# Expert weights in two-row pieces, features in a strided order, in a two-block transformer kernel

## The chip, the cores and the metric

The kernel runs on one core of a Trainium2 chip. The metric is the device time of one execution in microseconds (us), the median of several runs.

## The reference, cut to what matters

A first block (two layers with three mixing branches) is followed by a second block, whose last part is a layer of 16 experts. Each expert takes the 64 tokens (`cap = 2 * 512 / 16`) that the router likes best. All arithmetic is float32; the 16 experts' three 1024 x 1024 matrices are 201 MB.

```python
def expert_choice_ffn(h, w_router, w_gate, w_up, w_down):
    ...
    aff = jax.nn.softmax((h @ w_router).astype(jnp.float32), axis=-1)
    gates, idx = lax.top_k(aff.transpose(0, 2, 1), cap)
    xe = h[bidx, idx]
    hg = jnp.einsum('becd,edf->becf', xe, w_gate)
    hu = jnp.einsum('becd,edf->becf', xe, w_up)
    y = jnp.einsum('becf,efd->becd', jax.nn.silu(hg) * hu, w_down)
    y = y * gates[..., None].astype(y.dtype)
    return jnp.zeros_like(h).at[bidx, idx].add(y)
```

## The kernel before, in words

A planner of the language orders each engine's instructions and places the buffers; the kernel's text gives priorities and dependences. The change touches the last stage, `emit_moe`, which runs eight rounds (`q`), each with two experts (`e`). A round has these steps:

- The one-hot matrix (L1364, DVE) marks which token sits in which of the 128 slots of the pair.
- The gather (L1375, TensorE) multiplies it with the residual stream: for each block `k` of 128 features, four products, one for each tile of tokens. The stationary operand is `K.x[t][:, 128 columns]`, the moving one is the one-hot matrix. ACT (L1378) writes the result to `xe`, scaled by `n2` and shifted by `modc`, both per feature.
- `ffn` (L1387) is called for gate, up and down. For each `k` and each `e` it takes one tile of weights, 128 rows of the matrix, one row on a partition (4 KB each, 512 KB a tile), as moving operand. The stationary operand is 64 columns wide, so that expert 0 fills one half of the array's columns and expert 1 the other. In the code's order the two column halves `hf` of expert 0 come first, then those of expert 1.
- Four transposes for each half of the hidden layer (L1403) give `aT`, the stationary operand of the down products.
- The scatter (L1418) multiplies with the transposed one-hot matrix and adds to the output.

One float32 product is recorded as two weight loads (PEld) and two matmuls (PE), so a call of `ffn` has 32 products and 64 records, a gather 32 products and 64 records. The transposes have one record each.

The weights come on SP's queue from `wm` (L214, and through `wraw`, L173). The first 8 tiles (`NE`) have places of their own, the rest go round a ring of 28 tiles (`NW` 4 in `wring`, `NM` 24 in six tiles `wm0` to `wm5`), all 512 KB each. A place is loaded again when the products that read it are done.

Two older lines matter for reading the trace. `tm` (L743 to L753) makes token-major products from the transposed rows `hT`: `tm(0, ...)` takes 128 neighbouring columns as stationary operand, `tm(1, ...)` (L783) every fourth column, `slice(t, None, 4)`; nothing else differs between the two. `Mod.group` (L918) has four strips `j` of the array's columns with one product each, strip by strip in the code.

## Time and profile before

| | us |
|---|---|
| median of 3 runs | 2271.3 (2269.49 to 2281.24) |
| span of the profiled execution | 2273.9 |
| of it, the eight rounds of the experts, from the first gather | 494.2 |
| one round in the middle | 61.75 |

In the rows below, PE is TensorE's matmuls, PEld its weight loads, DVE, ACT and POOL the other engines, SPq the queue on which SP issues transfers. `out<-in` are the program's names for tiles, `x60` is a count, "idle before" is how long the engine had nothing to do and who ended that. A matmul record is longer than the step from one to the next, since matmuls are pipelined: rates are read from the start times.

### The profile page before, as it was taken

Reading aid. Unit: us, or ns where it says so; the run is one execution under the profiler, and the core shown is the slowest. Engines: PE = TensorE matmul, PEld = TensorE weight load, DVE = VectorE, ACT = ScalarE, POOL = GpSimd, SP = SyncE. Lnnn points to the kernel's source line nnn. Section 1 sums busy time; section 2 is a strip of 40 time slices with the busy share of each in tenths; the row PEclk is TensorE's granted clock in tenths of the full one; section 3 lists DMA queues with packets and bytes.
Section 4 is the critical chain, followed back from the end, with each engine's and each line's share of the span. In section 5 each row is a group of like instructions: output and inputs, shape, how many; then the busy total and the mean of one; then the engine's idle time right before and its main releaser. Section 6 shows DMA issues by size and latency. Waiting matters only on the chain. (4 is left out here: it accounts for less than half of the span.)

```text
span 2273.9 us, 31807 instructions
## 1 busy us (share of the span) xinstructions
PE 2128.9 (94%) x12273; PEld 1439.3 (63%) x12273; DVE 1258.6 (55%) x2406; ACT 980.0 (43%) x1849; POOL 429.6 (19%) x344
## 2 busy tenths in 40 slices
PE   6998999999999899999899999999999799999999
PEld 6754667668886676668767777676677444444443
DVE  5688855655569877645867474757464322222221
ACT  4454545444544464444577584857532011101110
POOL 2132233112222323202141140323110000000000
PEclk9999999899999999999999999999999799999999
DMA  6254251043321111034210202011146699999996
GB/s 203 84 171 146 77 168 57 18 158 107 94 87 38 38 38 47 22 124 153 73 51 31 73 20 75 24 61 43 52 157 257 263 401 409 409 409 409 409 409 267
DMA packets 114335, 348.48 MB, mean 153 GB/s; under 512 B 19820, under 2 KB 20604, under 8 KB 114184
## 3 DMA queue, kind: packets, MB, share of 16 engines
q1 hardware_dynamic: 110152, 340.51, 40.7%
q10 hardware_dynamic: 4032, 5.95, 0.8%
q8 instruction: 97, 1.59, 0.3%
q14 instruction: 54, 0.44, 0.1%
HBM read 332.70 MB, written 10.56 MB: 151 GB/s over the span
## 5 line engine op out<-in xcount | busy, mean ns | idle before, releaser
L193 POOL TENSOR_TENSOR wL<-wring,wH 128x1024 fp32r<-128x1024 f32 x68 | 167.2, 2459 | 702.0 <-ACT wH L190 498.8
L190 ACT ACTIVATE wH<-wring 128x1024 fp32r<-128x1024 f32 x137 | 144.1, 1059 | 133.5 <-PE bm L199 96.5
L1387 PE MATMUL bm<-wm,xe 128*64 128x512 f32 x848 | 185.4, 593 | 0.0
L199 PE MATMUL bm<-hT0H,wH 128*128 128x512 f32 x380 | 158.7, 418 | 2.9 <-ACT wH L190 2.9
L199 PE MATMUL bm<-hT1L,wH 128*128 128x512 f32 x380 | 159.8, 421 | 0.0
L199 PE MATMUL bm<-hT0L,wH 128*128 128x512 f32 x380 | 159.6, 420 | 0.0
L199 PE MATMUL bm<-hT0H,wL 128*128 128x512 f32 x380 | 158.6, 417 | 0.0
L199 PE MATMUL bm<-hT1H,wL 128*128 128x512 f32 x380 | 156.5, 412 | 0.0
L199 PE MATMUL bm<-hT1H,wH 128*128 128x512 f32 x380 | 156.0, 411 | 0.0
L1387 PEld LDWEIGHTS bm<-wm,xe 128*64 128x64 f32 x848 | 75.2, 136 | 106.4 <-issue 99.6
L193 DVE TENSOR_TENSOR wL<-wring,wH 128x1024 fp32r<-128x1024 f32 x69 | 92.2, 1337 | 74.4 <-ACT wH L190 66.4
L344 DVE TENSOR_TENSOR Z<-bz,perm 128x512 f16<-128x512 f32 x168 | 108.6, 684 | 36.7 <-PE bz L323 35.6
L1364 DVE TENSOR_SCALAR OH<-phA,perm 128x64 f32<-128x64 f32 x128 | 30.2, 309 | 136.4 <-PE bz L1375 105.7
L1387 PE MATMUL bm<-wm,aT 128*64 128x512 f32 x432 | 102.3, 602 | 0.7
L354 ACT ACTIVATE XX<-bz 128x512 f16<-128x512 f32 x168 | 101.3, 610 | 3.6 <-PE bz L323 3.6
L323 PEld LDWEIGHTS <-XX 128*128 128x128 f16 x1008 | 63.6, 99 | 59.5 <-issue 27.9
L351 ACT ACTIVATE XX<-bz 128x512 f16<-128x512 f32 x140 | 85.2, 608 | 16.7 <-PE bz L323 14.9
L199 PEld LDWEIGHTS bm<-hT0H,wH 128*128 128x128 f32 x380 | 72.8, 192 | 19.4 <-issue 4.2
L199 PEld LDWEIGHTS bm<-hT0L,wH 128*128 128x128 f32 x380 | 72.6, 191 | 17.5 <-issue 5.7
L199 PEld LDWEIGHTS bm<-hT1L,wH 128*128 128x128 f32 x380 | 71.9, 189 | 18.2 <-issue 5.9
L199 PEld LDWEIGHTS bm<-hT1H,wL 128*128 128x128 f32 x380 | 71.9, 189 | 18.1 <-issue 5.3
L199 PEld LDWEIGHTS bm<-hT0H,wL 128*128 128x128 f32 x380 | 72.6, 191 | 15.5 <-issue 3.3
(815 smaller groups left out, 4922.6 us busy)
## 6 DMA issues: line engine op xcount, KB each, us to landing
wm<-in_w_up SPq DMA_DIRECT2D x112, 512.0 KB
wm<-in_w_down SPq DMA_DIRECT2D x108, 512.0 KB
wm<-in_w_gate SPq DMA_DIRECT2D x100, 512.0 KB
wring<-in_win SPq DMA_DIRECT2D x95, 512.0 KB
wring<-in_w_ada SPq DMA_DIRECT2D x48, 512.0 KB
wring<-in_w_gate SPq DMA_DIRECT2D x20, 512.0 KB
wring<-in_w_down SPq DMA_DIRECT2D x20, 512.0 KB
wring<-in_w_out SPq DMA_DIRECT2D x16, 512.0 KB
```

The source lines that it names most:

```text
L190: d = self.A.activation(out=hi, in_=t, func=AF.Copy)
L193: (eng or self.V).tensor_tensor(out=lo, in0=t, in1=hi.bitcast(F32), op=ALU.subtract)
L199: self.T.matmul(out, a[i], b[j], start=(start and n == 0), stop=(stop and n == 2))
L323: T.matmul(b[:, u], lhs[:, u], rhs if len(rhs.shape) == 2 else rhs[:, u], start=True, stop=True)
L344: V.tensor_tensor(out=z, in0=mm(HL[j][0], X[j]), in1=lv(systems[j], l, 0), op=ALU.mult)
L351: A.activation(out=X[j], in_=mm(XT[j], Z[j]), func=AF.Copy)
L354: A.activation(out=XT[j], in_=b, func=AF.Copy)
L1364: V.tensor_scalar(out=y[:, t, 64 * e:64 * e + 64], in0=K.c("iota")[:, 1:65], scalar1=slot[:, t, x:x + 1], scalar2=scale(t, x), op0=ALU.is_ ...
L1387: T.matmul(bb[hf][s], lhs[:, k, s], w[:, hf * 512:(hf + 1) * 512], start=(k == 0), stop=(k == 7))
```

## The change

A transfer of expert weights now brings 256 rows: partition `p` gets two adjacent rows of the matrix (8 KB in one piece, 1 MB a transfer). Of each half of 512 rows, partition `p` holds the rows `4p` to `4p + 3`, the first two in one transfer and the other two in the next. So a block of features `k` is no longer 128 neighbouring features but every fourth one of a half: the gather's stationary operand and the transposes' input are read with a step of four elements. The scale and shift of `xe` are fetched in that order by four small transfers into `nx`, with one DVE operation. In `ffn` a tile now holds two blocks `k`, and the loops are `k0`, `e`, `k`, `hf`, so all eight records of expert 0 come ahead of the eight of expert 1. The ring keeps its bytes: half as many places, twice as large. Comments and docstrings go.

```diff
-NW = 4
+NR = 4
+NW = 2
...
-NM = 24
-NM1 = 8
-NC = 4
-NE = 8
+NM = 12
+NM1 = 4
+NC = 2
+NE = 4
...
     def wm(self, src, pool):
...
-            t = pool.tile([128, 1024], F32, name="we", bufs=NE)
+            t = pool.tile([128, 2, 1024], F32, name="we", bufs=NE)
         elif j < 0:
-            return self.wraw(src)
+            t = self.wring[:, 2 * (j + NW):2 * (j + NW) + 2]
         else:
             if first and j % NC == 0:
-                self.wms = getattr(self, "wms", []) + [pool.tile([128, NC, 1024], F32, name="wm%d" % (j // NC))]
+                self.wms = getattr(self, "wms", []) + [pool.tile([128, NC, 2, 1024], F32, name="wm%d" % (j // NC))]
...
+    nx = K.small("n2x", 24).rearrange("p (j k) -> p j k", j=3)
+    for j, o in enumerate((4096, 3072)):
+        for h in range(2):
+            nc.sync.dma_start(nx[:, j, 4 * h:4 * h + 4], K.mod.flat[:, o + 512 * h:o + 512 * h + 512].rearrange("o (p k) -> (o p) k", k=4))
+    V.scalar_tensor_tensor(out=nx[:, 2], in0=nx[:, 0], scalar=1.0, in1=K.v2[:, _V2["n2x"][0]:_V2["n2x"][0] + 8], op0=ALU.add, op1=ALU.mult)
...
+    strided = lambda k: slice(512 * (k // 4) + k % 4, 512 * (k // 4) + 512, 4)
...
-                    T.matmul(b[:, j], K.x[t][:, (k0 + j) * 128:(k0 + j + 1) * 128], OH[:, t], start=(t == 0), stop=(t == 3))
+                    T.matmul(b[:, j], K.x[t][:, strided(k0 + j)], OH[:, t], start=(t == 0), stop=(t == 3))
...
-                A.activation(out=xe[:, k], in_=b[:, j], func=AF.Identity, scale=n2[:, k:k + 1], bias=modc[:, 24 + k:25 + k])
+                A.activation(out=xe[:, k], in_=b[:, j], func=AF.Identity, scale=nx[:, 2, k:k + 1], bias=nx[:, 1, k:k + 1])
...
-            for k in range(8):
+            for k0 in range(0, 8, 2):
                 for e in range(2):
-                    w = K.wm(a[name][2 * q + e, k * 128:(k + 1) * 128], P2["wm"])
+                    rows = a[name][2 * q + e, 512 * (k0 // 4):512 * (k0 // 4) + 512].rearrange("(p k) n -> p k n", k=4)
+                    w = K.wm(rows[:, k0 % 4:k0 % 4 + 2], P2["wm"])
                     s = slice(64 * e, 64 * e + 64)
-                    for hf in range(2):
-                        T.matmul(bb[hf][s], lhs[:, k, s], w[:, hf * 512:(hf + 1) * 512], start=(k == 0), stop=(k == 7))
+                    for k in (k0, k0 + 1):
+                        for hf in range(2):
+                            T.matmul(bb[hf][s], lhs[:, k, s], w[:, k - k0, hf * 512:(hf + 1) * 512], start=(k == 0), stop=(k == 7))
...
-                T.transpose(b[:, j], hid[hf][:, j * 128:(j + 1) * 128], K.ident)
+                T.transpose(b[:, j], hid[hf][:, j::4], K.ident)
```

## Rows read from the trace of the kernel before

**Rows 1.** Busy time by engine over three rounds; last columns: clock, DMA share, GB/s.

```profile
1779.67:1842.38 62.71, 61.17 (x290) 31.80 (x291) 13.37 (x35) 6.11 (x13) 0.00 (x0) 0.95 0.71 277
...
2025.27:2087.02 61.75, 59.99 (x285) 27.19 (x285) 13.09 (x31) 6.10 (x13) 0.00 (x0) 1.00 1.03 409
...
2210.52:2273.90 63.38, 57.88 (x236) 23.74 (x236) 15.31 (x23) 2.83 (x5) 0.00 (x0) 1.00 0.71 282
```

**Rows 2.** DMA view, 1900 to 2200 us: total, and the queue with the weights.

```profile
DMA packets 33642, 122.69 MB, mean 409 GB/s; under 512 B 3732, under 2 KB 3732, under 8 KB 33624
...
q1 hardware_dynamic: 33624, 122.45, 102.4%
```

**Rows 3.** Waits, 1850 to 2200 us: total us, times, longest.

```profile
PEld bm L1387 <- DMA wm<-in_w_down: 1.6, 7, 0.2
...
PEld bm L1387 <- DMA wm<-in_w_up: 0.7, 3, 0.2
...
PEld bm L1387 <- DMA wring<-in_w_down: 0.2, 1, 0.2
```

**Rows 4.** Timeline of PE, one round: start us, us, operation, count, idle before.

```profile
2025.27 7.11 PE L1418 MATMUL bg<-yg,oT 128*128 128x512 f32 x16 [0.90 <-DVE yg L1409]
...
2046.09 13.96 PE L1387 MATMUL bm<-wm,xe 128*64 128x512 f32 x64
2060.80 1.25 PE L1403 MATMUL bt<-perm,hid 128*128 128x128 f32 x8 [0.76 <-DVE hid L1398]
...
2068.24 1.94 PE L1387 MATMUL bm<-wm,aT 128*64 128x512 f32 x8
2070.11 1.60 PE L1375 MATMUL bz<-OH,x 128*128 128x128 f32 x12
2071.65 1.94 PE L1387 MATMUL bm<-wm,aT 128*64 128x512 f32 x8
```

**Rows 5.** Timeline of SP's queue: the last weights, and one row fetched earlier.

```profile
1771.72 0.33 SPq L245 DMA_DIRECT2D gt<-modb  x1
...
2232.21 9.28 SPq L214 DMA_DIRECT2D wm<-in_w_down  x8
```

**Rows 6.** Chain that ended last: its last three pieces of `ffn`.

```profile
2217.62 27.71 PE bm L1387 x128
2247.45 1.94 PE bm L1387 x8
2249.98 12.26 PE bm L1387 x56
```

**Rows 7.** Timeline of PEld: `tm(1)`, every fourth column; one load a row.

```profile
54.06 0.33 PEld L199 LDWEIGHTS bm<-wH,hT0H 128*128 128x128 f32 x1
...
57.56 0.33 PEld L199 LDWEIGHTS bm<-wH,hT0H 128*128 128x128 f32 x1
```

**Rows 8.** Timeline of PEld: `tm(0)`, neighbouring columns; one load a row.

```profile
30.02 0.19 PEld L199 LDWEIGHTS bm<-wH,hT0H 128*128 128x128 f32 x1
...
31.79 0.19 PEld L199 LDWEIGHTS bm<-wH,hT1H 128*128 128x128 f32 x1
```

**Rows 9.** Timeline of PEld: the second round's gather, 59 loads in a row.

```profile
1842.22 6.67 PEld L1375 LDWEIGHTS bz<-OH,x 128*128 128x128 f32 x59 [0.24 <-issue]
```

**Rows 10.** Timeline around the first round's gather, all engines.

```profile
1760.20 1.74 DVE L1324 SCALAR_TENSOR_TENSOR perm<-lg,perm 128x16 f32<-128x16 f32 x8 [0.78 <-PE lg L1300]
...
1779.67 10.08 PE L1375 MATMUL bz<-OH,x 128*128 128x128 f32 x64 [0.98 <-DVE OH L1364]
1783.46 0.81 ACT L1378 ACTIVATE xe<-bz,perm 128x128 f32<-128x128 f32 x2 [18.15 <-PE bz L1375]
...
1789.67 2.85 PE L1387 MATMUL bm<-we,xe 128*64 128x512 f32 x12
```

**Rows 11.** Timeline of PE: one step of the modulation's products.

```profile
137.87 1.04 PE L918 MATMUL bm<-wring,perm 128*1 128x512 f32 x8
```

## The prediction

> **What bounds the kernel now.** I began with the clock and the busy shares by stage, since the change touches only the eight rounds of the experts, 494.2 us of 2273.9. In a middle round TensorE is busy for 59.99 of 61.75 us at full clock, and the transfers run at 409 GB/s with all engines taken [rows 1]. Both look full, so the busy shares don't say which one sets the pace. Three other views do. The DMA view says the rate is steady at 409 GB/s over 300 us [rows 2]: a round's 48 tiles, 25.17 MB, need 25.17 / 0.409 = 61.5 us, almost exactly the round. The waits say that in 350 us TensorE waited for weights 11 times, 2.5 us in all, never over 0.2 us [rows 3]. And at the end the last weights are issued by 2241.5 us [rows 5], while the last call of `ffn` runs from 2247.45 to 2262.2 [rows 6]: TensorE is behind the transfers, not ahead. So TensorE sets the pace; transfers follow by a hair. The timeline of one round shows what fills it: scatter 7.11, `ffn` for gate and up 13.96 each, 0.90 and 0.76 idle, transposes 1.25, then down and the next gather in turns [rows 4]. Whatever makes TensorE's work longer lengthens the round; what shortens the transfers finds nobody waiting.

> **Faster transfers.** Half as many transfers, pieces of 8 KB for 4 KB. No row has such pieces for weights, so their rate is bounded by what it can do: a faster rate gains at most the 2.5 us of [rows 3], which I book as a gain, since a longer round also gives it. A slower rate costs nothing until 25.17 MB take longer than the new round, below 25.17 / 69.4 = 363 GB/s. The ring keeps its bytes. A place comes free after 1 MB of work, later than now, but the first weights lie ready long before the first gather.

> **The gather's stationary operand, every fourth column.** The trace has this very form elsewhere: `tm(1)` loads 128 columns with a step of four floats, `tm(0)` 128 neighbouring ones, all else alike. In `tm(1)` 15 loads take 57.56 - 54.06 = 3.50 us, 0.233 us each, recorded as 0.33 [rows 7]. In `tm(0)` 15 loads take 1.77 us, 0.118 each, recorded as 0.19 [rows 8]. The gather has 0.19 us loads too, 59 of them in 6.67 us, so (6.67 - 0.19) / 58 = 0.112 us each [rows 9]. Its matmuls are as short as the step, so nothing covers a longer load: I take 0.233 for 0.112, 0.121 us more on each of 64 loads, 7.8 us a round. For the seven rounds after the first: 7 x 64 x 0.121 = 54.2 us. The first gather runs partly at half clock and takes 10.08 us [rows 1, 10]; 64 x 0.233 = 14.9 gives +4.8, and +9.8 if its first 21 loads take double. All of this is on TensorE, which sets the pace.

> [...]

> **Transposes.** Eight a round have the hidden layer with a step of four as stationary operand; now they take 1.25 us [rows 4]. No row shows a strided transpose. The bounds are nothing and the same 0.233 for each: 8 x 0.233 = 1.87, with a tail of 0.2 some 2.05, +0.8 a round and +6.4 in all. I take the upper end, since it is the same kind of load. They stand alone between up and down, so it counts fully.

> **Order and turns in `ffn`.** Eight records of `ffn` between two pieces of gather take 1.87 us from start to start, a piece of gather of 12 takes 1.54 [rows 4]. Undisturbed, 8 records take 13.8 / 64 x 8 = 1.73 and 12 loads 1.34: one turn costs 0.14 + 0.20 = 0.34 us. Five rounds have such turns, 8 pieces of down each. With two blocks a tile I expect 4 pieces, 4 x 0.34 x 5 = 6.8 us less; if the planner keeps the pieces it is 0. I take half, -3.4.

> The 64 records in 13.96 us also show that expert 0's and expert 1's records run side by side on the two halves of the columns: a record alone takes 0.44 (16 in 7.11) [rows 4], so 64 in a row would take 28. Yet the code has four of expert 0, then four of expert 1, so the array starts expert 1's over three waiting ones. Now eight stand ahead. Rows 11 show 8 records on four strips in 1.04 us, four at once, though the fourth strip's first stands six places behind the first strip's: it reaches that far at least. I take 0 for the new order; the other end is the second rival.

> If matmuls could start only in the order of the code, expert 1's first could run beside expert 0's eighth at the earliest: 14 steps of 0.43 us for each 16 records where 8 do now, 2.6 us on each of 96 pairs of tiles, +248 us. The records that overtake others in [rows 4, 11] speak against it.

> [...]

> **The four small transfers and their users.** They go on SP's queue, behind weights: a row of the modulation now leaves at 1771.72 [rows 5]. ACT's `xe` waits for them, and behind it `ffn`. The first `xe` runs at 1783.46 and `ffn` starts at 1789.67 after the gather [rows 10]; the gather, which gets longer, hides them. I take 0. If the DVE operation were queued ahead of the router's chain, which starts at 1760.20 [rows 10], DVE would wait up to the transfers' landing near 1780, and the one-hot matrix and gather behind it: +20.

> **Sum.** 54.2 + 4.8 + 6.4 - 3.4 - 2.5 = 59.5 us, 2333.4 for the profiled 2273.9. The median of the runs is 2.6 lower, 2271.3, so 2331. The bounds: 54.2 + 4.8 - 6.8 - 2.5 = 49.7 below (transposes free) and 54.2 + 9.8 + 6.4 = 70.4 above. The planner may order the earlier stages a little differently; I allow 5 us either way, for which no row stands: 2316 to 2347.

> **Rivals.** First, on the other side: the load's second half is hidden, because the gather's loads are the two parts of plain float32 and those of `tm` are not, or because the array fetches them ahead. Then TensorE keeps its rounds, and only the turns and waits change: 2271.3 - 9.3 = 2262, at worst 2271. It decides if the new gather's loads stay under 0.112 us. For it: both forms record 0.19 us unstrided. Against: that likeness says that they read alike, and `tm`'s matmuls, whose step is 0.118, did not hide 0.233. Chance 0.09; half hidden, near 2300, 0.06.

> Second: the two experts no longer run fully side by side. If the array reaches no further than the six places of rows 11, expert 1 starts two records late, 0.86 us, at each of five starts a round: 40 x 0.86 = +34, 2365. If the planner puts gather between expert 0's eight and expert 1's, down takes 28 for 14 us in five rounds: +69, 2400. Chance 0.17 together. The strict order above, 2580, has 0.03.

> Third: the DVE operation stalls the router's chain, 2351. Chance 0.03. That transfers in pieces fall below 363 GB/s and bound the round, 0.02.

> **How the numbers follow.** The forecast, 2331, has 0.60. From 2305 to 2395 lie the forecast with its bounds, the third rival and most of the second: some 0.8. A measurement tells about 0.5%, 11 us, from no change. Faster by more needs under 2260, a little less than the first rival's lowest: 0.03. Within: the rest of the first rival, 0.06. Slower: 0.91.

> **What would show it.** The gather's loads recorded near 0.33 us and 64 in 15 us; rounds of 69 to 70 us; mean DMA rate in a round near 25.17 / 69.4 = 363 GB/s with gaps, where 409 stood without; transposes near 2 us; `ffn` for gate and up still near 14 us each. Loads of 0.19 us would make it wrong, as would 28 us for a call of `ffn`.

## The result, and the profile after

The changed kernel takes 2456.1 us (median), the kernel before 2276.3 in the same comparison: 1.0786 times as long, 95% interval 1.074 to 1.0832. I had forecast 2331, from 2305 to 2395. The direction was right, the size was not. In the profiled executions 2454.7 stands against 2273.9, 180.8 us more.

First the windows view: from the start to the first gather, and from there to the end, for before and after, and then one middle round of after. The columns are those of [rows 1].

```profile
0.00:1779.67 1779.67, 1652.13 (x10002) 1215.99 (x10002) 1154.72 (x2170) 931.24 (x1745) 429.59 (x344) 0.97 0.27 92
1779.67:2273.90 494.23, 476.77 (x2272) 223.30 (x2272) 103.90 (x238) 48.76 (x104) 0.00 (x0) 0.99 0.95 375
```

```profile
0.00:1839.36 1839.36, 1679.43 (x9997) 1224.40 (x10002) 1162.80 (x2171) 932.47 (x1745) 426.09 (x344) 0.96 0.26 88
1839.36:2454.70 615.34, 603.73 (x2272) 305.40 (x2272) 106.24 (x238) 49.02 (x104) 0.00 (x0) 0.99 0.76 304
2233.42:2312.89 79.47, 77.94 (x285) 38.54 (x284) 13.38 (x30) 6.10 (x13) 0.00 (x0) 1.00 0.80 317
```

The loss has two places. 59.7 us are lost before the first gather, in stages that the change's text does not touch. The other 121.1 are lost in the rounds: one takes 79.47 us where [rows 1] has 61.75, TensorE is busy for 77.94 of it, and the transfers bring 317 GB/s where they brought 409. So the bound is the one I had named; TensorE just has more to do than I had counted.

The timeline of PE over that round, to be laid beside [rows 4]:

```profile
2233.42 16.06 PE L1398 MATMUL bm<-wm,xe 128*64 128x512 f32 x64
2250.89 4.13 PE L1398 MATMUL bm<-wm,xe 128*64 128x512 f32 x13 [1.41 <-DVE hid L310]
...
2266.88 1.60 PE L1414 MATMUL bt<-perm,hid 128*128 128x128 f32 x8
...
2268.85 5.42 PE L1398 MATMUL bm<-wm,aT 128*64 128x512 f32 x16
2274.20 6.33 PE L1384 MATMUL bz<-OH,x 128*128 128x128 f32 x26
2280.46 5.42 PE L1398 MATMUL bm<-wm,aT 128*64 128x512 f32 x16
2285.81 5.87 PE L1384 MATMUL bz<-OH,x 128*128 128x128 f32 x24
2291.61 5.42 PE L1398 MATMUL bm<-wm,aT 128*64 128x512 f32 x16
2296.96 3.53 PE L1384 MATMUL bz<-OH,x 128*128 128x128 f32 x14
2300.42 5.42 PE L1398 MATMUL bm<-wm,aT 128*64 128x512 f32 x16
2305.86 7.10 PE L1429 MATMUL bg<-yg,oT 128*128 128x512 f32 x16
```

Read by start times, against the middle round of before (2025.27 to 2087.02):

| part of a round, us | before | after | more |
|---|---|---|---|
| scatter | 7.03 | 7.03 | 0 |
| gate, to the start of up | 13.79 | 17.47 | 3.68 |
| up, to the start of the transposes | 14.71 | 15.99 | 1.28 |
| the gather's pieces, 64 loads | 8.34 | 15.52 | 7.18 |
| down's pieces, with the wait ahead of the scatter (0.90 before, none after) | 15.94 | 21.49 | 5.55 |
| transposes of the hidden layer and of the one-hot matrix | 1.94 | 1.97 | 0.03 |

The gather is what I had forecast. Gate, up and down are not: 64 records of gate take 16.06 us where [rows 4] has 13.96, up then waits 1.41, and a piece of down of 16 records takes 5.35 where two pieces of 8 took 3.74.

The timeline of PEld shows why: one such piece of down, its 16 loads, rows grouped by the gaps between them.

```profile
2109.90 0.19 PEld L1398 LDWEIGHTS bm<-wring,aT 128*64 128x64 f32 x2 [0.17 <-issue]
2110.38 0.14 PEld L1398 LDWEIGHTS bm<-wring,aT 128*64 128x64 f32 x1 [0.29 <-issue]
2110.81 0.14 PEld L1398 LDWEIGHTS bm<-wring,aT 128*64 128x64 f32 x1 [0.29 <-issue]
2111.24 0.14 PEld L1398 LDWEIGHTS bm<-wring,aT 128*64 128x64 f32 x1 [0.29 <-issue]
2111.67 0.19 PEld L1398 LDWEIGHTS bm<-wring,aT 128*64 128x64 f32 x3 [0.29 <-issue]
2112.10 0.19 PEld L1398 LDWEIGHTS bm<-wring,aT 128*64 128x64 f32 x2 [0.24 <-issue]
2112.53 0.19 PEld L1398 LDWEIGHTS bm<-wring,aT 128*64 128x64 f32 x2 [0.24 <-issue]
2113.01 0.14 PEld L1398 LDWEIGHTS bm<-wring,aT 128*64 128x64 f32 x1 [0.29 <-issue]
...
2114.30 0.14 PEld L1398 LDWEIGHTS bm<-wring,aT 128*64 128x64 f32 x1 [0.29 <-issue]
```

A step is 0.43 us (2110.38 to 2110.81), and the load of a record that waits comes one step ahead of its matmul: in the run with sixteen of one expert, below, expert 0's last three loads start at 2056.44, 2056.87 and 2057.30, its last three matmuls at 2056.87, 2057.30 and 2057.73. For four steps one load comes at a time: expert 0 is alone. At 2111.67, as expert 0's fifth record starts and its sixth is loaded, expert 1's first two loads appear. For four steps both run; then expert 1 is alone for four. That is 12 steps for 16 records, where four and four in turn need 8. When expert 1's first gets through, expert 0's sixth, seventh and eighth are still waiting: it has overtaken three. (Both experts' tiles lie in `wring` here, so which load is whose is inferred from the gaps; a run below has the two in different tiles.)

### The profile page after: what moved, and what is told of

Same layout as the page of the kernel before. It is cut to its first block, busy times and chain, and to the rows that moved or that the text cites. A ratio compares the mean times of both kernels' runs of the same rounds, so it can differ in the third digit from the quotient of the medians.

```text
span 2454.7 us, 31438 instructions
## 1 busy us (share of the span) xinstructions
PE 2283.2 (93%) x12269; PEld 1529.8 (62%) x12273; DVE 1269.0 (52%) x2407; ACT 981.5 (40%) x1849; POOL 426.1 (17%) x344
## 5 line engine op out<-in xcount | busy, mean ns | idle before, releaser
L1398 PE MATMUL bm<-wm,xe 128*64 128x512 f32 x848 | 221.7, 598 | 6.2 <-DVE hid L310 6.2
L1398 PEld LDWEIGHTS bm<-wm,xe 128*64 128x64 f32 x848 | 81.4, 136 | 133.5 <-issue 119.0
L1398 PE MATMUL bm<-wm,aT 128*64 128x512 f32 x432 | 140.7, 598 | 0.0
L1384 PEld LDWEIGHTS bz<-OH,x 128*128 128x128 f32 x512 | 121.4, 328 | 16.3 <-issue 14.5
L1384 PE MATMUL bz<-OH,x 128*128 128x128 f32 x512 | 124.4, 402 | 1.0 <-DVE OH L1371 1.0
L1387 ACT ACTIVATE xe<-bz,perm 128x128 f32<-128x128 f32 x64 | 25.8, 453 | 218.8 <-PE bz L1384 210.1
L610 ACT ACTIVATE PT<-bt 128x128 f32<-128x128 f32 (+3 forms) x112 | 48.0, 430 | 123.1 <-PE bt L608 113.5
L1398 PEld LDWEIGHTS bm<-wm,aT 128*64 128x64 f32 x432 | 45.9, 136 | 75.3 <-issue 73.3
```

The source lines that it names most:

```text
L610: K.A.activation(out=PT[:, :n], in_=b[:, :n], func=AF.Copy)
L1384: T.matmul(b[:, j], K.x[t][:, strided(k0 + j)], OH[:, t], start=(t == 0), stop=(t == 3))
L1398: T.matmul(bb[hf][s], lhs[:, k, s], w[:, k - k0, hf * 512:(hf + 1) * 512], start=(k == 0), stop=(k == 7))
```

## The experiments

Three theories came out of the two traces. *Strided loads*: 0.121 us more on each load of the gather. *Three waiting*: a record of the other half of the columns overtakes at most three waiting ones, so the order k0, e, k, hf lets expert 1 start four steps late. *Buffers*: in the program of the changed kernel sixteen tiles of the earlier stages (`PT`, `P`, `iacc`, `iq`, `iqy`, `rl`, `rraw`, `sth`, `xn` of the first block, `kz`, `rz`, `sq` of its RWKV branch, `P`, `cy`, `ghi`, `lsq` of the second block) get one buffer where the kernel before gets two. The planner chooses these numbers for the whole program, and the order of nearly all engines differs with them. (The expectations say 15, for 15 names.)

All kernels, with the names that the expectations use; the first two columns of times are from one profiled execution each, the others the median time and its ratio to the kernel before:

| kernel | first gather, us | from there to the end | time | ratio, 95% interval |
|---|---|---|---|---|
| before | 1779.7 | 494.2 | 2276 to 2280 | 1 |
| after | 1839.4 | 615.3 | 2456.1 | 1.0786 (1.074 to 1.0832) |
| single buffers alone (before1) | 1847.6 | 495.0 | 2344.6 | 1.0307 (1.0281 to 1.0333) |
| after, buffers given back (after2) | 1779.7 | 615.3 | 2397.2 | 1.0541 (1.0507 to 1.0575) |
| step of four alone (stride4) | 1776.1 | 554.1 | 2337.1 | 1.0269 (1.024 to 1.0298) |
| sixteen of one expert (order16) | 1787.9 | 701.3 | 2480.1 | 1.0907 (1.0868 to 1.0946) |
| buffers back, order undone (kfirst2) | 1781.5 | 587.7 | 2366.4 | 1.0387 (1.035 to 1.0425) |
| step of two, order undone (stride2k2) | 1841.1 | 530.4 | 2373.3 | one run |
| no strided load, order undone (xperm2) | 1778.3 | 531.5 | 2309.8 | 1.0147 (1.0118 to 1.0176) |
| step of two, the change's order (order2) | 1783.0 | 559.3 | 2344.8 | 1.0288 (1.0246 to 1.033) |
| both experts in one transfer (both2) | 1779.4 | 512.4 | 2293.8 | 1.0063 (1.0041 to 1.0086) |
| the same, two fixed pairs (both3) | 1781.0 | 490.9 | 2269.6 | 0.9970 (0.9951 to 0.9989) |

### Where the 59.7 us before the rounds come from

Single buffers alone, in the kernel before:

```diff
+class Bufs:
+    def tile(self, shape, dtype, name, **kw):
+        if name in self.names:
+            kw["bufs"] = self.n
+        return self.pool.tile(shape, dtype, name=name, **kw)
...
-    P["sp"] = E(tc.tile_pool(name="sp"))
+    P["sp"] = Bufs(E(tc.tile_pool(name="sp")), 1, "PT P iacc iq iqy rl rraw sth xn")
...
```

> The kernel before, with the buffers of 15 tiles of the earlier stages held at one where the planner gave them two: exactly those that have one in the changed kernel. Nothing in the experts' stage is touched. Theory 'buffers' (the 59.7 us that the changed kernel loses before the first gather come from these single buffers): first gather near 1839 us (1830 to 1848) instead of 1779.7, the eight rounds still near 494, time near 2272 + 60 = 2332 (2320 to 2342). Rival 'own parts' (the loss comes from something that the change itself brings, its four small transfers, its vector of 8 more columns, its larger transfers or a lower clock): first gather at 1780, time 2265 to 2280.

The same edit with 2 for 1, in the changed kernel:

> The changed kernel, with these 15 tiles held at two buffers, as the planner gave them in the kernel before. Theory 'buffers': first gather near 1780 us (1772 to 1788), the eight rounds still 615, time near 2456 - 60 = 2396 (2386 to 2408). Rival 'own parts': first gather near 1839, time 2450 to 2462.

Both went as *buffers* said, in both directions. The windows view up to the first gather, for the first kernel and then for the second:

```profile
0.00:1847.60 1847.60, 1689.75 (x10001) 1229.76 (x10002) 1162.55 (x2169) 932.13 (x1745) 426.60 (x344) 0.96 0.26 87
```

```profile
0.00:1779.70 1779.70, 1653.15 (x10002) 1216.70 (x10002) 1154.20 (x2171) 932.23 (x1745) 429.17 (x344) 0.97 0.27 91
```

With the sixteen tiles at two, the changed kernel reaches its first gather at 1779.7 us, as the kernel before does, and its rounds keep their 615.3. That the two agree to the tenth is luck: these are single executions, and the executions of one kernel differ by some 20 us. The medians give 58.9 us back (2456.1 against 2397.2). With the tiles at one, the kernel before loses 67.9 us there, 8 more than the changed kernel (its time is 2.6 us above the expected range), and its rounds stay. Of the changed kernel's 59.7, TensorE is idle for 32.4 (159.9 against 127.5) and busy 27.3 longer at a granted clock of 0.96 for 0.97. Which of the sixteen cost most was not tried. What makes the planner choose is narrowed only by the programs: with tiles of weights of 512 KB the sixteen had two buffers (step of four alone, sixteen of one expert), with 1 MB one, unless they were held. Why is open.

### What the strided order costs alone

```diff
-                    T.matmul(b[:, j], K.x[t][:, (k0 + j) * 128:(k0 + j + 1) * 128], OH[:, t], start=(t == 0), stop=(t == 3))
+                    T.matmul(b[:, j], K.x[t][:, strided(k0 + j)], OH[:, t], start=(t == 0), stop=(t == 3))
...
-                    w = K.wm(a[name][2 * q + e, k * 128:(k + 1) * 128], P2["wm"])
+                    rows = a[name][2 * q + e, 512 * (k // 4):512 * (k // 4) + 512].rearrange("(p k) n -> p k n", k=4)
+                    w = K.wm(rows[:, k % 4], P2["wm"])
...
-                T.transpose(b[:, j], hid[hf][:, j * 128:(j + 1) * 128], K.ident)
+                T.transpose(b[:, j], hid[hf][:, j::4], K.ident)
```

> The kernel before with the strided order alone: every fourth feature in the gather and the transposes, the four small transfers, but tiles of 512 KB with one row of 4 KB on a partition and the loops k, e, hf as before. Theory 'strided loads': 0.233 us for each of the gather's 64 loads where 0.112 stood, so a round's gather 15 us for 7, 7.7 more a round and 4.8 in the first, and 0.35 a round for the transposes, all of it on TensorE: from the first gather to the end 494 + 59 + 3 = 556 us (545 to 570), first gather at 1780, time near 2335. Rival 'hidden': gather loads near 0.11 us, time within 0.5% of the kernel before. Rival 'transfers': the rounds lengthen because pieces that lie 16 KB apart come slower, which would show as waits of the products for weights, and the gather's loads would then not account for the rise.

From the first gather to the end it took 554.1 us, 59.9 more than before. Timelines of PEld (60 loads of the second gather) and PE (transposes, in a later round):

```profile
1843.66 14.27 PEld L1382 LDWEIGHTS bz<-OH,x 128*128 128x128 f32 x60 [0.24 <-issue]
```

```profile
2023.70 1.34 PE L1411 MATMUL bt<-perm,hid 128*128 128x128 f32 x8 [0.77 <-DVE hid L1406]
```

(14.27 - 0.33) / 59 = 0.236 us a load, where `tm(1)` in [rows 7] gave 0.233 and [rows 9] 0.112. The eight transposes take 1.34 for 1.25: next to nothing. The longest wait for weights stayed at 0.2 us.

The transposes' loads did become longer. The timelines of PEld, before and then here:

```profile
2060.80 0.42 PEld L1403 LDWEIGHTS bt<-perm,hid 128*128 128x128 f32 x4 [1.65 <-DVE hid L1398]
2061.40 0.42 PEld L1403 LDWEIGHTS bt<-perm,hid 128*128 128x128 f32 x4 [0.18 <-DVE hid L1398]
```

```profile
2023.70 1.15 PEld L1411 LDWEIGHTS bt<-perm,hid 128*128 128x128 f32 x8 [1.65 <-DVE hid L1406]
```

One is recorded as 0.209 us for 0.140; from start to start it takes (1.15 - 0.21) / 7 = 0.134 us where (0.42 - 0.14) / 3 = 0.093 stood. Over eight that is some 0.3 us, but the 0.18 that the second four used to wait is gone.

### What the order costs alone

In the kernel before, with the loops k0 in (0, 4), e, four k, hf:

```diff
-            for k in range(8):
+            for k0 in range(0, 8, 4):
                 for e in range(2):
-                    w = K.wm(a[name][2 * q + e, k * 128:(k + 1) * 128], P2["wm"])
...
+                    for k in range(k0, k0 + 4):
+                        w = K.wm(a[name][2 * q + e, k * 128:(k + 1) * 128], P2["wm"])
```

> The kernel before with another order of the products alone: four tiles of expert 0, then four of expert 1, so 16 records of expert 0 stand ahead of expert 1's. Theory 'three waiting' (a record of the other half of the columns overtakes at most three that still wait): expert 1's first starts 12 steps of 0.43 us after expert 0's first, and so does each later group; gate and up in a row take 3 x 24 + 12 + 16 = 100 steps, 43 us where 27.7 stood; a call of down alone 52 steps, 22.4 us where 13.9 stood, more if the planner puts gather between. Rounds longer by 15 + 8 or more: from the first gather to the end 494 + 190 = 680 us (650 to 740). Rival 'six places' (overtaking reaches six waiting records): 9 steps late, 79 steps for gate and up, 34 us, rounds 494 + 90. Rival 'side by side' (no limit that matters): gate and up keep 27.7 us and the time stays. Rival 'strict order' (no overtaking): 15 steps late, 30 a group, 121 steps, 52 us.

The timeline of PE has one call of `ffn` by itself, and that of PEld a place where the two experts' tiles lie in different buffers (`wm` expert 0, `wring` expert 1), so that they can be told apart:

```profile
2074.55 22.70 PE L1388 MATMUL bm<-wm,xe 128*64 128x512 f32 x64 [0.61 <-DVE hid L309]
```

```profile
2052.09 0.19 PEld L1388 LDWEIGHTS bm<-wm,xe 128*64 128x64 f32 x2 [0.76 <-issue]
...
2056.01 0.14 PEld L1388 LDWEIGHTS bm<-wm,xe 128*64 128x64 f32 x1 [0.29 <-issue]
2056.44 0.14 PEld L1388 LDWEIGHTS bm<-wm,xe 128*64 128x64 f32 x1 [0.29 <-issue]
2056.44 0.19 PEld L1388 LDWEIGHTS bm<-wring,xe 128*64 128x64 f32 x2
2056.87 0.14 PEld L1388 LDWEIGHTS bm<-wm,xe 128*64 128x64 f32 x1 [0.24 <-issue]
2056.93 0.14 PEld L1388 LDWEIGHTS bm<-wring,xe 128*64 128x64 f32 x1
2057.30 0.14 PEld L1388 LDWEIGHTS bm<-wm,xe 128*64 128x64 f32 x1 [0.23 <-issue]
```

A call takes 22.70 us; three waiting gives 22.4, six places would have given 43 steps (18.5), no limit 13.9, the strict order 61 (26.2). Expert 1's first loads come at 2056.44, together with the third-last load of expert 0. In the planner's program all of expert 0's 16 still stand ahead of expert 1's, as in the code, so by that program the overtaking in the trace is TensorE's and not the planner's. The rounds took 701.3, inside the expected 650 to 740. The order alone, with nothing else changed in the code, makes the kernel 9% slower at this length.

Then the changed kernel with buffers given back and the order undone:

```diff
             for k0 in range(0, 8, 2):
+                ws = []
                 for e in range(2):
...
+                    ws.append(K.wm(rows[:, k0 % 4:k0 % 4 + 2], P2["wm"]))
+                for k in (k0, k0 + 1):
+                    for e in range(2):
...
```

> The changed kernel with the 15 tiles held at two buffers, and with the order of the products undone: both experts' tiles are fetched, then the loops run k, e, hf, so again four records of expert 0 and four of expert 1 take turns; strided loads and transfers of 1 MB stay. Theory 'three waiting': the 61 us that the rounds of the changed kernel take more than those of the kernel before with the strided order alone (615.3 against 554.1) go: gate and up back from 33.5 to near 28 us, eight records of down in a row side by side, from the first gather to the end 554 us (545 to 562), first gather at 1780, time near 2335. Rival 'transfers': these 61 us come from the 1 MB transfers (a place comes free later, products wait for weights), and the rounds stay near 615.

587.7 us, not 554: 27.6 of the 61 us came back. Gate and up are back (13.95 a call). Down is not; the timeline of PE:

```profile
2126.33 3.53 PE L1394 MATMUL bz<-OH,x 128*128 128x128 f32 x14
2129.79 3.65 PE L1410 MATMUL bm<-wm,aT 128*64 128x512 f32 x12
2133.37 3.07 PE L1394 MATMUL bz<-OH,x 128*128 128x128 f32 x12
2136.37 1.93 PE L1410 MATMUL bm<-wring,aT 128*64 128x512 f32 x4
2138.23 3.07 PE L1394 MATMUL bz<-OH,x 128*128 128x128 f32 x12
```

The planner lets expert 0's first four records run as soon as its tile is there, puts a piece of gather behind them, and then the other twelve. Four records alone take 1.86 us, twelve 3.58: 5.44 for 16, even more than the order it was to mend. The transfers were not to blame; TensorE never waited for weights. This is a split by the planner, of the kind that my second rival had priced at +69; here it cost 33.6 (587.7 - 554.1).

To have the order's price in the form of the change, at no cost for the gather's loads, I kept the order and took a step of two (next part):

> The order of the changed kernel alone, at no cost for the loads: transfers of 1 MB with 8 KB pieces, two adjacent rows of each 256 on a partition (a step of two floats, whose loads took 0.2 us recorded, as without a step), the 15 tiles held at two buffers, and the loops k0, e, k, hf of the changed kernel, so eight records of expert 0 stand ahead of expert 1's. Theory 'three waiting': gate and up in a row take 4 + 64 steps of 0.43 us and what stands between, 33.5 us as in the changed kernel; a piece of down of 16 records takes 5.35 us; from the first gather to the end 494 + 61 = 555 us (545 to 565); first gather near 1780; time near 2336. Rival 'transfers' (part of these 61 us comes from the 1 MB transfers or from the strided gather that pushes down's pieces apart): rounds well below 545 or products waiting for weights.

559.3 us, 68.4 above the last kernel of the table, which has the same loads, turns of four and fixed accumulators. Down's pieces take 5.35 us, and between gate and up stands the 1.41 of the changed kernel. So the 68.4 hold a second thing beside the order, a wait for accumulators: the waits view has it in five rounds, with the same figures in the changed kernel, here for the latter:

```profile
PE bm L1398 <- DVE hid L310: 6.2, 5, 1.4
```

The last kernel of the table, whose accumulators are fixed, has none of it.

### A step of two

```diff
-    strided = lambda k: slice(512 * (k // 4) + k % 4, 512 * (k // 4) + 512, 4)
+    strided = lambda k: slice(256 * (k // 2) + k % 2, 256 * (k // 2) + 256, 2)
...
-                    rows = a[name][2 * q + e, 512 * (k0 // 4):512 * (k0 // 4) + 512].rearrange("(p k) n -> p k n", k=4)
+                    ws.append(K.wm(a[name][2 * q + e, 128 * k0:128 * k0 + 256].rearrange("(p k) n -> p k n", k=2), P2["wm"]))
```

> The kernel kfirst2 but without the held buffers, and with another strided order: partition p holds two adjacent rows of each 256, again 8 KB in one piece and 1 MB a transfer, so that the gather and the transposes read every second feature. The early stages are those of the changed kernel (first gather near 1839). If any step costs the same as a step of four, the loads take 0.233 us, the gather 15 us and the rounds 554. If a load's time goes with the stretch of memory that it spans, a step of two is between: near 0.15 us, rounds near 515. If a step of two is as free as none, 0.112 us and rounds near 494.

The timeline of PEld, one gather:

```profile
1902.74 7.03 PEld L1384 LDWEIGHTS bz<-OH,x 128*128 128x128 f32 x59 [0.23 <-issue]
```

(7.03 - 0.20) / 58 = 0.118 us a load: a step of two costs 0.006, a step of four 0.124. The rounds took 530.4, not 494, because this kernel has the 4 and 12 split too. The first gather at 1841.1 fits the single buffers. So of the three cases that I had set out, the last came, free but for 5%. Why the gather's loads take 0.118 us with a step of two and 0.236 with a step of four is not shown. The transposes' loads go another way: with a step of two eight of them take 1.15 us, as with a step of four:

```profile
1938.39 1.15 PEld L1415 LDWEIGHTS bt<-perm,hid 128*128 128x128 f32 x8 [1.65 <-DVE hid L1410]
```

### Without strided loads, and what is left of the change

GpSimd writes the residual stream once in the new order, so that the gather reads neighbours:

```diff
+    acc, xs = K.x, [hp.tile([128, 1024], F32, name="mxo%d" % t) for t in range(4)]
+    for t in range(4):
+        for h in range(2):
+            y, x = (v[t][:, 512 * h:512 * h + 512] for v in (xs, K.x))
+            G.tensor_copy(y.rearrange("p (j i) -> p i j", j=4), x.rearrange("p (i j) -> p i j", j=4))
```

> The kernel kfirst2 without any strided load: GpSimd writes the residual stream once, before the first gather, into the places of the output's sum with the features in the new order, so the gather reads 128 neighbouring columns again; the sum is kept in the stream itself; the hidden layer's product is written in the new order by DVE, so the transposes read neighbouring columns too. What is left of the change is the larger pieces. Theory 'strided loads' with 'three waiting': the rounds are back at 494 us; they can gain the 2.5 us of the waits for weights and up to 6.8 us of turns, 485 to 494, first gather near 1780, time 2263 to 2276: the transfers find nobody waiting. Rival 'transfers bound': if the rounds before were set by the transfers at 409 GB/s, faster pieces shorten them by over 2%, below 484. Rival 'transfers slow': rounds longer than 500 with waits for weights.

531.5 us, 56.2 less than the same kernel with a step of four, but not 485 to 494: the split of down again, which I had not allowed for, and some 5 us more of waiting for DVE ahead of the transposes (10.7 for 6.1), since DVE writes the hidden layer in the new order.

So I gave the planner no place to split: one transfer brings both experts' pair of tiles.

```diff
+                w = K.wm(a[name][2 * q:2 * q + 2, 128 * k0:128 * k0 + 256].rearrange("e (p k) n -> p e k n", k=2), P2["wm"])
+                for k in (k0, k0 + 1):
+                    for e in range(2):
...
+                            T.matmul(bb[hf][s], lhs[:, k, s], w[:, e, k - k0, hf * 512:(hf + 1) * 512], start=(k == 0), stop=(k == 7))
```

> The same pieces of 8 KB and the step of two floats, the 15 tiles at two buffers, but one transfer of 2 MB brings the pair of tiles of both experts, and the loops are k, e, hf. The planner then has no place where one expert's weights are there and the other's not, and its order keeps eight products of down together, four pieces a round, where it put pieces of gather between four and twelve records before. All three losses are gone: first gather near 1780, rounds 494 less up to 2.5 us of waits for weights and 4 turns x 0.34 us x 5 rounds = 6.8, so 485 to 494, time 2264 to 2276 by the run's own kernel before at 2276. Rival 'places': a place of 2 MB comes free later and fewer weights lie ready before the first gather, products wait for weights, rounds above 500. Rival 'transfers bound': the rounds before were set by the transfers, and faster pieces bring them below 484.

512.4 us: down's four pieces are whole and take 3.64 us, no product waits for weights (so it isn't the rival of the places), and yet 18 us more than the upper end are left. The timeline of PE between gate and up, and the windows view of the microseconds after:

```profile
1983.45 3.65 PE L1407 MATMUL bm<-wm,xe 128*64 128x512 f32 x16
1989.07 12.27 PE L1407 MATMUL bm<-wm,xe 128*64 128x512 f32 x48 [1.97 <-DVE hid L320]
```

```profile
1990.00:1991.00 1.00, 1.00 (x4) 0.25 (x2) 0.00 (x0) 0.00 (x0) 0.00 (x0) 0.50 1.00 418
1991.00:1992.00 1.00, 1.00 (x4) 0.23 (x1) 0.00 (x0) 0.00 (x0) 0.00 (x0) 0.50 1.00 418
1992.00:1993.00 1.00, 1.00 (x6) 0.39 (x5) 0.00 (x0) 0.00 (x0) 0.00 (x0) 0.50 1.03 418
```

Up waits 1.97 us for DVE, which still reads gate's result: in this program one of up's two accumulators has the same place as one of gate's. (So it is in the changed kernel, with its 1.41, and not in the kernel before, which has no such wait.) Afterwards the granted clock is 0.50 for some 3.4 us (0.80 over the microsecond before the three shown, 0.99 over the one behind them), and 48 records take 12.27 us where they took 10.57. There are six such waits, in six of the eight rounds. After the first (up to 1926.04) the clock stayed at 1.00; after each of the other five the records took 1.70 us longer, as here, and the clock over its round was 0.97 or 0.98. That makes 6 x 1.97 + 5 x 1.70 = 20.3 us.

```diff
+    banks = [[K.pm.tile([128, 512], F32, name="bm", bufs=4) for _ in range(2)] for _ in range(2)]
...
-            bb = [K.pm.tile([128, 512], F32, name="bm", bufs=4) for _ in range(2)]
+            bb = banks.pop(0)
+            banks.append(bb)
```

> The kernel both2 with the accumulators of the three calls of ffn taken in turn from two fixed pairs, so that up no longer takes the pair from which the same round's gate is still being read. In both2 TensorE stood 1.97 us between gate and up in six rounds, and in most of them the granted clock was 0.97 after it and the following products took 1.75 us longer. Theory 'pair of accumulators': both go, a round takes 64.7 - 3.7 = 61.0 us, where it took 61.75 in the kernel before, from the first gather to the end 486 to 494 us, time 2265 to 2277, no more than 0.5% from the kernel before, for TensorE's busy time stays and the transfers run at 411 to 414 GB/s with all engines taken, 61 us a round. Rival: the wait and the lower clock have another cause (the hidden layer itself comes late), and the time stays near 2293.

Wait and low clock are gone (1.00 from 1850 us to the end), and the rounds are at 490.9 us, 21.5 less. One round in the windows view:

```profile
2033.53:2094.33 60.80, 59.22 (x286) 28.39 (x285) 13.11 (x30) 5.95 (x13) 0.00 (x0) 1.00 1.01 415
```

This is the idea of the change without its three costs, in another form (a step of two, 2 MB a transfer, fixed accumulators), and it takes 0.3% less time than the kernel before (ratio 0.9951 to 0.9989). A round takes 60.80 us for 61.75. TensorE is busy 59.22 for 59.99, most of which is down in four pieces for eight; no product waited for weights. The transfers run at 415 GB/s for 409 with all engines taken, and 25.17 MB at that rate need 60.7 us. So the larger pieces are worth 1.5% of the rate. In this form there was hardly more to be had: the transfers fill the round, and TensorE nearly does.

## Why the prediction was wrong

- **What bounds the kernel** held. Rounds are TensorE's, after as before. **Faster transfers** held too: nobody waited for weights, so the change could gain next to nothing on its own side.
- **The gather's strided operand** held: 0.236 us a load by 0.233 forecast. Alone it added 59.9 us to the rounds where I had 59.0 for loads and 6.4 for transposes. **Transposes** was a term mis-sized: 0.09 us for eight, some 0.7 in all, for 6.4. I had taken them for the same kind of load as the gather's. They do become longer, but to 0.134 us from start to start and not to 0.233, and a wait of 0.18 between the two halves went. Why they cost less than the gather's, and the same with a step of two as with four, is open.
- **Turns in `ffn`**: four pieces came, of which I had booked half the gain. By the last kernel the four saved turns and the waits are worth 0.95 us a round.
- **The order of the two experts** is the step that failed: "I take 0 for the new order". I read in [rows 11] that the fourth strip's first record stood six places behind the first strip's, and called these six places of reach. But of those six, three had started, one on each of the other strips; only three waited. So no row before showed more than three overtaken, and I counted the wrong records; that a fourth wasn't overtaken only the runs show (5.35 us for 16 records with eight ahead, 22.70 for 64 with sixteen). With eight ahead expert 1 starts four steps late. My second rival took six places and so two late records, 34 us, for the price. It cost 61.2 us (615.3 - 554.1): in the round shown 5.55 on down's pieces, about 2 each on gate and up by the late start (0.76 of up's lies in the wait for the hidden layer, which went), and 1.41 in the wait between gate and up, which came with the planner's new accumulators. That wait isn't the order's own; it is 6.2 of the 61.2 us, and why the planner shares a place in some of these programs is open.
- **The earlier stages** is the other step that failed: "I allow 5 us either way, for which no row stands". 59.7 us were lost there, and two opposite runs show that the number of buffers does it. No row of the trace before could have shown it. The program could: the planner's numbers of buffers are there to be read before anything runs.
- **The four small transfers and their users**: 0, as taken. The kernel with them and the small tiles reached its first gather at 1776.1 us.

The three costs make 59.7 + 59.9 + 61.2 = 180.8, the whole difference of the spans. They must, since the last two are taken from the kernel before to the step of four alone and from there to the changed kernel; what speaks for the third by itself is the run with the change's order and a step of two (555 expected, 559.3 measured). The forecast had the second; for the first it had 5 us of room, and for the third nothing. Without the first the change would have taken 2397.2, still just above the range.

## What to carry to other kernels

Two chains that share TensorE by column halves should take turns in groups of four records: four ran side by side (64 records in 13.96 us), eight and sixteen did not (16.06 and 22.70), and lengths between were not run. Write that order out, and give the planner no moment at which one chain can run and the other not. Before a change of tile sizes is timed, compare the numbers of buffers that the planner chooses for the whole program, and hold those that mattered. The gather's stationary operand could be read with a step of two floats (0.118 us a load for 0.112), not of four (0.236); and if the stream that a change makes faster isn't waited for, its gain is at most the waits that the trace shows.
